# Mixture-of-experts encoder: the last expert's last 512 columns brought to their tokens by products with a matrix of ones

## The chip, the cores and the metric

One core of one Trainium2 chip. The metric is device microseconds (us) for one execution of the whole program. TensorE is called PE here (PEld is its weight load), VectorE DVE, ScalarE ACT, GpSimd POOL, and SyncE SP; SPq and POOLq are the queues in which SP and POOL issue transfers.

## The reference, cut to what matters

A two-layer encoder on 512 tokens of width 1024. Attention and the dense feed-forward of layer 0 are the same in both kernels. What the change touches is the end of layer 1: a mixture of 8 experts, of which each token takes 2.

```python
def _moe(h, router_w, router_b, w1, w3, w2):
    logits = (hf @ router_w) + router_b
    top_logits, top_idx = lax.top_k(logits, 2)
    gates = softmax(top_logits)
    # each expert e on the rows x of its tokens:
    y = (silu(x @ w1[e]) * (x @ w3[e])) @ w2[e]      # 1024 -> 2816 -> 1024
    out[token] += gate * y                           # two experts per token
...
x = layernorm(ALPHA * x + g2 * moe(h), ln2_g, ln2_b)  # the output, 512 x 1024
```

## The kernel before

**Places.** The router ranks the experts by how many tokens they have and gives each a *place* with a fixed number of rows, `SLOT = [336, 320, 128, 128, 64, 64, 64, 64]`; what doesn't fit goes to 7 spare blocks of 128 rows, computed at the very end under a condition (`tc.If(n_ovv > 0)`). Each of the 4 blocks of 128 tokens has, for its 2 experts, a row number in `dst` (as float in `dstf`) and a gate in `gw`.

**Two lanes.** `lane_big` computes places 0 and 1, `lane_small` the other six; their steps are interleaved by hand by shares of work. Every float32 product is made of three (`mm3`) or two products of parts, high (`wh`) and low (`wl`); ACT makes the high part of each weight tile (L111) and DVE the low (L113). Place 1 (320 rows, blocks of 128, 128 and 64) is the last work of the program. Its last product, with the second half of the inner dimension, is cut by columns into `PIECES = [(0, 512), (512, 256), (768, 256)]`. `out_turned` (L1504) computes a piece with columns on the partitions and adds it into `part` on DVE (L1525, scaled by `g2col`). `turn_back` (L1529) transposes it on PE (L1533), copies it from the PSUM bank on ACT (L1535) and stores it in DRAM (L1542), in `ybuf`, which is three tensors, one for each piece.

**Combine.** When a piece's rows are stored, `Final.combine(i)` (L1665) fetches, for each of 4 blocks of tokens and each of the 2 experts, 128 rows of that piece by an indirect transfer from POOL (L1679); DVE multiplies by the gate and adds to the residual `us` (L1681) and takes statistics (L1684). That is 8 gathers for a piece, 24 in all. For the last piece the normalisation follows, block by block: mean and variance (L310), the root on ACT (L312, L313) and DVE (L314 to L317), one pass over 128x1024 on DVE (L1687), and a second one: for two of the blocks on ACT (L1689) and POOL (L1690), for the other two on DVE (L1692). Then the block is stored (L1693).

**Order.** At build time a planner writes one list of instructions for each engine, with costs of its own; a line of the source that is ready in its plan can move ahead of earlier ones, unless `order(after, before)` forbids it. On the chip each engine runs its list in that order. In `combine` the adds are ordered behind the last write of `part` (`order(j, first)`, `first = last_out[0]`). Tiles with one `tag` share `bufs` buffers: `ye` and `hs` have 3 each, the PSUM tag `pt` has 2 and `ps` 6.

Of the kernel before, what the change touches and what calls it, by code (L numbers as in the profile page):

```python
# [18 lines left out]
D = 1024  # L19
# [37 lines left out]
def build(tc, I, out, dbg=None, upto=99):  # L57
# [1008 lines left out]
    G.memset(zero, 0.0)  # L1066
    zeros = [(y, SLOT_ROWS + i * P) for i in range(N_OVER) for y in ybuf]
    js = ExitStack()
    jobs = mod_steps(js.enter_context(tc.tile_pool(name="jp", bufs=1, side="right")), [(0, 5, None), (1, 1, 1.0), (1, 0, 0.0), (1, 2, None), (1, 4, 1.0), (1, 3, 0.0), (1, 5, None)])
    for f in range(FT):  # L1070
        pp_ = []
        for _ in range(4):
            next(jobs, None)
        for y, r in zeros[f:f + 1]:
            SP.dma_start(y[r:r + P, :], zero[:, :y.shape[1]])
        for w in ("ffn_w1", "ffn_w3"):
# [398 lines left out]

    last_out = [None]
    g2col = modcol[1, 5]

    def out_part(ew2, lhs, c0, nc_, store, late=None):
# [19 lines left out]
        z = pz if gl is not None else halves(pz, nc_)  # L1499
        last_out[0] = V.tensor_tensor(y[:m, :nc_], z[:m, :nc_], g2row[:m, c0:c0 + nc_], op=OP.mult)  # L1500
        store(0, c0, nc_, y[:m, :nc_])
        yield 1

    def out_turned(ew2, lhs, part, c0, nc_, fs, first):  # L1504
# [3 lines left out]
        for c in range(c0, c0 + nc_, 256):  # L1508
# [11 lines left out]
            for i in range(2):  # L1520
                m = c // P + i
                if first:
                    A.activation(part[:, m, :], pz[i][:, :n], AF.Copy, scale=g2col[:, m:m + 1])
                else:
                    last_out[0] = V.scalar_tensor_tensor(part[:, m, :], pz[i][:, :n], g2col[:, m:m + 1],  # L1525
                                                         part[:, m, :], op0=OP.mult, op1=OP.add)
# [11 lines left out]
    def stores(row):  # L1538
        def f(i, c0, nc_, y):
            for (b0, bn), buf in zip(PIECES, ybuf):  # L1540
                if c0 <= b0 < c0 + nc_:
                    SP.dma_start(buf[row(i, y.shape[0]), :], y[:, b0 - c0:b0 - c0 + bn])  # L1542
        return f
# [75 lines left out]
    def lane_big():  # L1619
        for s, nxt in zip(lanes[0], lanes[0][1:] + (None,)):  # L1620
# [29 lines left out]

    class Final:

        def prepare(self):
# [10 lines left out]

        def combine(self, i):  # L1665
            c0, n = PIECES[i]
            last = i == len(PIECES) - 1
            table = exp_table() if last else None
            ys = []
            for tag, k in ((("geh", 5), ("gel", 3)), (("xeh", 4), ("xel", 4)), (("xg", 4), ("xg", 4)))[i]:  # L1670
                y = xp.tile([P, k, n], F32, name=nm("yg"), tag=tag, bufs=XG if tag == "xg" else 1)
                ys += [y[:, j, :] for j in range(k)]
            first = last_out[0]
            for t in range(NT):
                u = self.us[t]
                uc = u[:, c0:c0 + n]
                for k in range(2):
                    y = ys[2 * t + k]
                    G.indirect_dma_start(out=y, out_offset=None, in_=ybuf[i],  # L1679
                                         in_offset=bass.IndirectOffsetOnAxis(ap=dst[:, t, k:k + 1], axis=0))  # L1680
                    j = V.scalar_tensor_tensor(uc, y, gw[:, k, t:t + 1], uc, op0=OP.mult, op1=OP.add)  # L1681
                    if first is not None:
                        order(j, first)
                V.bn_stats(self.sts[t][:, i, :], uc)  # L1684
                if last:
                    mean, r = ln_stat(xp, self.sts[t], table)
                    V.scalar_tensor_tensor(u, u, mean, self.lg, op0=OP.subtract, op1=OP.mult)  # L1687
                    if t < 2:
                        A.activation(u, u, AF.Copy, scale=r)  # L1689
                        G.tensor_tensor(u, u, self.lb, op=OP.add)  # L1690
                    else:
                        V.scalar_tensor_tensor(u, u, r, self.lb, op0=OP.mult, op1=OP.add)  # L1692
                    SP.dma_start(out[0, t * P:(t + 1) * P, :], u)  # L1693

# [20 lines left out]
    fin.combine(len(PIECES) - 1)  # L1715

# [3 lines left out]
    with tc.If(n_ovv > 0):  # L1720
        with tc.For_i(0, n_ovv, 1) as i:
# [14 lines left out]
        last_out[0] = None  # L1736
        again = Final()
        again.prepare()
        for i in range(len(PIECES)):
            again.combine(i)  # L1740
    ms.close()
# [25 lines left out]
```

## Time and profile before

| | |
|---|---|
| time before, median of 3 runs | 2538.1 us (2535.07 to 2540.49) |
| the profiled execution: its own time | 2537.35 us |
| its span, first to last instruction | 2535.5 us |
| outside the span | 1.85 us |
| busy: PE / DVE / ACT / POOL | 96% / 70% / 56% / 17% |
| mean granted clock of PE | 0.986 of full speed |

The span counts from the first instruction of the profiled execution; what lies around it, 1.85 us, is the difference to that execution's own time. Times in the rows below are us from the span's start. PE is busy nearly always, but a share over the whole span says nothing of the end, where PE has no work left.

### The profile page before, as it was taken

What the parts mean: (1) busy time and instruction counts of PE and PEld (TensorE: products, weight loads), DVE (VectorE), ACT (ScalarE), POOL (GpSimd) and SP (SyncE); (2) the same over time, 40 slices, a digit from 0 to 9 for tenths busy, and PEclk for the clock granted to TensorE, in tenths of its full rate; (3) what the DMA queues carried; (4) which work ended last, traced back from release to release, by engine and by line L of the source; (5) the groups of instructions that cost most, each with busy time, mean ns of one, the idle gap of its engine ahead of it and who ended that gap; (6) DMA issues with size and microseconds to landing.
All of it is one profiled execution on the core that took longest, in us unless ns stands there. A gap on an engine that the chain in (4) does not pass through costs nothing.

```text
span 2535.5 us, 37048 instructions
## 1 busy us (share of the span) xinstructions
PE 2436.4 (96%) x13124; PEld 2081.7 (82%) x13124; DVE 1779.1 (70%) x2788; ACT 1432.5 (56%) x2320; POOL 430.0 (17%) x393
## 2 busy tenths in 40 slices
PE   8999999998999999999999997999999999999994
PEld 6878877787788888878877876888899999999994
DVE  3688776647665335687775366977788888888875
ACT  3577774223222224677764225666677777777761
POOL 1423330001000502323326004400000000000004
PEclk9999999999999999999999998999999999999997
DMA  8322225746866433222226329998999999999993
GB/s 228 92 59 71 73 74 191 229 137 213 281 217 194 150 100 111 75 67 72 79 67 196 96 75 276 313 338 275 315 318 297 323 286 319 333 303 331 291 337 122
DMA packets 453210, 502.20 MB, mean 198 GB/s; under 512 B 19314, under 2 KB 322920, under 8 KB 453016
## 3 DMA queue, kind: packets, MB, share of 16 engines
q1 hardware_dynamic: 437616, 453.64, 57.1%
q0 software_dynamic: 13888, 45.30, 5.1%
q8 instruction: 105, 1.72, 0.3%
q10 hardware_dynamic: 1512, 0.81, 0.1%
q14 instruction: 89, 0.73, 0.1%
HBM read 474.95 MB, written 24.74 MB: 197 GB/s over the span
## 4 chain that ended last, share of the span: by engine, by line
PE 79%; DVE 7%; DMA 6%; ACT 5%; issue 2%; POOL 1%; SPq 0%; ACTq 0%; DVEq 0%; POOLq 0%
PE ps L127 21%; PE ps L128 20%; PE ps L129 20%; PE ps L1371 5%; PE ps L1372 5%; PE pt L444 2%; DMA ws<-in_moe_w 2%; DMA mst<-in_w_ada 1%; DVE wl L113 1%; ACT wh L111 1%; PE ps L732 1%; PE ps L733 1%; DMA ol<-o_dram 1%; DVE ps L745 1%; DMA ws<-in_w_in 1%
## 5 line engine op out<-in xcount | busy, mean ns | idle before, releaser
L111 ACT ACTIVATE wh<-ws 128x1024 fp32r<-128x1024 f32 (+3 forms) x786 | 779.0, 1011 | 688.5 <-PE ps L128 342.9
L113 DVE TENSOR_TENSOR wl<-ws,wh 128x1024 fp32r<-128x1024 f32 (+3 forms) x712 | 836.2, 1193 | 356.4 <-ACT wh L111 348.5
L129 PE MATMUL ps<-hTh,wl 128*128 128x512 f32 (+1 forms) x904 | 347.5, 385 | 4.4 <-DVE wl L113 4.4
L128 PE MATMUL ps<-hTl,wh 128*128 128x512 f32 (+1 forms) x904 | 349.3, 387 | 0.8 <-POOL hTl L282 0.8
L127 PE MATMUL ps<-hTh,wh 128*128 128x512 f32 (+1 forms) x904 | 349.7, 387 | 0.1
L127 PE MATMUL ps<-x3h,wh 128*128 128x336 f32 (+1 forms) x704 | 221.2, 314 | 0.0
L129 PE MATMUL ps<-x3h,wl 128*128 128x336 f32 (+1 forms) x704 | 220.3, 313 | 0.0
L128 PE MATMUL ps<-x3l,wh 128*128 128x336 f32 (+1 forms) x704 | 219.9, 312 | 0.0
L113 POOL TENSOR_TENSOR wl<-ws,wh 128x1024 fp32r<-128x1024 f32 (+1 forms) x74 | 179.3, 2430 | 216.0 <-ACT wh L111 148.0
L129 PEld LDWEIGHTS ps<-hTh,wl 128*128 128x128 f32 x904 | 171.6, 190 | 37.9 <-DVE wl L113 5.3
L127 PEld LDWEIGHTS ps<-hTh,wh 128*128 128x128 f32 x904 | 171.6, 190 | 35.4 <-issue 2.9
L128 PEld LDWEIGHTS ps<-hTl,wh 128*128 128x128 f32 x904 | 171.5, 190 | 32.9 <-POOL hTl L282 2.0
L1371 PE MATMUL ps<-wh,xes 128*128 128x512 f32 (+1 forms) x384 | 143.3, 378 | 0.0
L1372 PE MATMUL ps<-wl,xes 128*128 128x512 f32 (+1 forms) x384 | 141.4, 374 | 0.0
L127 PEld LDWEIGHTS ps<-x3h,wh 128*128 128x128 f32 x704 | 132.3, 188 | 3.4
L128 PEld LDWEIGHTS ps<-x3l,wh 128*128 128x128 f32 x704 | 132.4, 188 | 3.0
L129 PEld LDWEIGHTS ps<-x3h,wl 128*128 128x128 f32 x704 | 132.1, 188 | 0.2
L127 PE MATMUL ps<-wh,hTh 128*128 128x256 f32 (+1 forms) x384 | 116.5, 305 | 1.8 <-DVE dq L519 1.1
L214 DVE SCALAR_TENSOR_TENSOR macc<-mst,condrep,macc 128x1024 f32<-128x1024 f32 x70 | 89.8, 1282 | 35.7 <-DMA mst<-in_w_ada 35.0
L128 PE MATMUL ps<-wl,hTh 128*128 128x256 f32 (+1 forms) x384 | 114.0, 298 | 0.8 <-DVE wl L113 0.8
L129 PE MATMUL ps<-wh,hTl 128*128 128x256 f32 (+1 forms) x384 | 113.4, 297 | 0.0
L124 DVE TENSOR_TENSOR pTl<-pt,pTh 128x512 fp32r<-128x512 f32 x128 | 86.5, 685 | 36.1 <-ACT pTh L123 35.5
(428 smaller groups left out, 5371.2 us busy)
## 6 DMA issues: line engine op xcount, KB each, us to landing
ws<-in_moe_w SPq DMA_DIRECT2D x492, 512.0 KB, 5.8
ws<-in_w_in SPq DMA_DIRECT2D x94, 512.0 KB, 3.9
mst<-in_w_ada SPq DMA_DIRECT2D x80, 512.0 KB, 4.8
ws<-in_ffn_w SPq DMA_DIRECT2D x66, 512.0 KB, 4.0
ws<-in_moe_w SPq DMA_DIRECT2D x48, 256.0 KB, 3.8
wa<-in_w_ada SPq DMA_DIRECT2D x16, 512.0 KB, 6.4
ws<-in_w_br_diff SPq DMA_DIRECT2D x16, 512.0 KB, 3.7
ws<-in_w_out SPq DMA_DIRECT2D x16, 512.0 KB, 3.8
```

Source lines behind the costliest of these rows:

```text
L111: A.activation(h, st, AF.Copy)
L113: i = eng.tensor_tensor(l, st, h, op=OP.subtract)
L124: V.tensor_tensor(l, src, h, op=OP.subtract)
L127: T.matmul(o, ah, bh, start=start, stop=False)
L128: T.matmul(o, ah, bl, start=False, stop=False)
L129: last_mm[0] = T.matmul(o, al, bh, start=False, stop=stop)
L214: i = V.scalar_tensor_tensor(acc, st, condrep[:, k, 0:1], acc, op0=OP.mult, op1=OP.add)
L444: T.transpose(pt[:, t * P:(t + 1) * P], tiles[t][:, k * P:(k + 1) * P], ident)
L732: T.matmul(scs[m], q[:, m, tt], k[:, m], start=True, stop=False)
L733: last_mm[0] = T.matmul(scs[m], q[:, m, tt], kl[:, m], start=False, stop=True)
L1371: T.matmul(o, xs, wh, start=start, stop=False)
L1372: T.matmul(o, xs, wl, start=False, stop=stop)
```

## The change

`ybuf` becomes two tensors of 512 columns (`BUFS`). The rows of place 1 in the second one are filled with zeros early (during the dense feed-forward of layer 0), so that a gather from it brings the other experts' part alone and need not wait for place 1. `others` issues 16 gathers of 512 columns, the second half's first; it also builds `ones`, three tiles of 128 x 512 with a one where a row of place 1 belongs to a token (compare on DVE, transpose on PE, copy on ACT), and `gate`, the gate of that token for place 1. `adds` does the adds of one half, interleaved with the steps of `out_turned` for the second and the third piece. `scatter` replaces `turn_back` and `combine` for these two pieces: it transposes the piece back, splits it into high and low, multiplies both with `ones` into PSUM (24 products of 256 columns a piece) and adds the sum times `gate` to `us`. The normalisation is done for two blocks at a time (`norm`), its last block stored in two halves. The rows of place 1 are still stored, behind that, for the conditional part, which repeats the combine with 16 gathers.

```diff
+BUFS = [(0, 512), (512, 512)]
-    ybuf = [dram.tile([N_ROWS, n], F32, name=f"ybuf{i}") for i, (_, n) in enumerate(PIECES)]
+    ybuf = [dram.tile([N_ROWS, n], F32, name=f"ybuf{i}") for i, (_, n) in enumerate(BUFS)]
...
-    zeros = [(y, SLOT_ROWS + i * P) for i in range(N_OVER) for y in ybuf]
+    zeros = [(y, SLOT_ROWS + i * P, P) for i in range(N_OVER) for y in ybuf]
+    zeros += [(ybuf[1], SLOT[0] + i, min(P, SLOT[1] - i)) for i in range(0, SLOT[1], P)]
...
-                    yield from out_turned(ew[2], g[1], part, c0, nc_, (FH, FT), False)
-                    turn_back(part, SLOT[s], c0, nc_, row_stores(s))
-                    if nxt is None and i > 0:
-                        fin.combine(i - 1)
+                        fin.others(s)
+                    work = out_turned(ew[2], g[1], part, c0, nc_, (FH, FT), False)
+                    if nxt is not None or i == 0:
+                        yield from work
+                        turn_back(part, SLOT[s], c0, nc_, row_stores(s))
+                    else:
+                        adds = fin.adds(2 - i, fin.ys[2 - i])
+                        for n in work:
+                            yield n
+                            next(adds, None)
+                        for _ in adds:
+                            pass
+                        fin.scatter(s, i, c0, part)
...
+        def gathers(self, i, idx, tags):
...
+            for t in range(NT):
+                for k in range(2):
+                    G.indirect_dma_start(out=ys[2 * t + k], out_offset=None, in_=ybuf[i],
+                                         in_offset=bass.IndirectOffsetOnAxis(ap=idx[:, t, k:k + 1], axis=0))
+            return ys
+
+        def others(self, s):
...
+            late = self.gathers(1, dst, (("geh", 5), ("gel", 3)))
+            self.ys = [self.gathers(0, dst, (("xeh", 2), ("xel", 2), ("xg", 2), ("xg", 2))), late]
...
+            for t in range(NT):
+                p1 = xp.tile([P, 512], F32, name=nm("ye"), tag="ye", bufs=YE)
+                V.tensor_scalar(p1[:, :n], rows[:, :n], dstf[:, t, 0:1], None, op0=OP.is_equal)
+                V.scalar_tensor_tensor(p1[:, :n], rows[:, :n], dstf[:, t, 1:2], p1[:, :n], op0=OP.is_equal, op1=OP.add)
+                pt = psum_t()
+                for b, m in enumerate(blocks(n)):
+                    T.transpose(pt[:m, b * P:(b + 1) * P], p1[:, b * P:b * P + m], ident)
+                for b, m in enumerate(blocks(n)):
+                    A.activation(self.ones[b][:m, t * P:(t + 1) * P], pt[:m, b * P:(b + 1) * P], AF.Copy)
+
+        def adds(self, i, ys):
+            c0, n = BUFS[i]
+            for t in range(NT):
+                first = last_split[0]
+                uc = self.us[t][:, c0:c0 + n]
+                for k in range(2):
+                    j = V.scalar_tensor_tensor(uc, ys[2 * t + k], gw[:, k, t:t + 1], uc, op0=OP.mult, op1=OP.add)
+                    if first is not None:
+                        order(j, first)
+                if i == 0:
+                    V.bn_stats(self.sts[t][:, 0, :], uc)
+                yield
+
+        def scatter(self, s, i, c0, part):
...
+                        T.transpose(pt[:m, (b - b0) * 256 + j * P:(b - b0) * 256 + (j + 1) * P],
+                                    part[:, c0 // P + j, b * P:b * P + m], ident)
+                split(h[:m, w], l[:m, w], pt[:m, w])
...
+            for t0 in range(0, NT, 2):
+                pz = psum()
+                for t in (t0, t0 + 1):
+                    o = pz[:, (t - t0) * 256:(t - t0 + 1) * 256]
+                    for b, (m, h, l) in enumerate(hl):
+                        one = self.ones[b][:m, t * P:(t + 1) * P]
+                        T.matmul(o, one, h, start=(b == 0), stop=False)
+                        T.matmul(o, one, l, start=False, stop=(b == len(hl) - 1))
+                    uc = self.us[t][:, c0:c0 + 256]
+                    V.scalar_tensor_tensor(uc, o, self.gate[:, t:t + 1], uc, op0=OP.mult, op1=OP.add)
+                    V.bn_stats(self.sts[t][:, i, :], uc)
+                if last:
+                    self.norm((t0, t0 + 1), 3, table)
...
+        def norm(self, ts, n, table):
...
+            for j, t in enumerate(ts):
+                u = self.us[t]
+                V.scalar_tensor_tensor(u, u, mv[:, j, 0:1], self.lg, op0=OP.subtract, op1=OP.mult)
+                if t < 2:
+                    A.activation(u, u, AF.Copy, scale=r[:, j:j + 1])
+                    G.tensor_tensor(u, u, self.lb, op=OP.add)
+                    SP.dma_start(out[0, t * P:(t + 1) * P, :], u)
+                else:
+                    for c in HALVES if t == NT - 1 else [(0, D)]:
+                        c = slice(c[0], c[0] + c[1])
+                        V.scalar_tensor_tensor(u[:, c], u[:, c], r[:, j:j + 1], self.lb[:, c], op0=OP.mult, op1=OP.add)
+                        SP.dma_start(out[0, t * P:(t + 1) * P, c], u[:, c])
```

## Rows read from the trace of the kernel before

**Rows 1.** Windows: length, busy us (instructions) of each engine, PE clock, DMA.

```profile
2476.60:2498.95 22.35, 22.35 (x153) 21.39 (x151) 12.07 (x18) 4.62 (x8) 10.88 (x11) 1.00 0.49 148
2498.95:2535.50 36.55, 1.37 (x8) 0.54 (x6) 23.09 (x53) 5.11 (x13) 19.03 (x16) 0.57 0.36 121
```

**Rows 2.** The chain that ended last, its end: start, us, what.

```profile
2492.63 3.75 DMA yg<-ybuf,r
...
2501.74 4.56 DMA ybuf<-ye
2507.09 1.19 POOL yg L1679
```

**Rows 3.** Timeline of PE: start, us (pipelined, so starts give the pace).

```profile
1284.05 0.28 PE L127 MATMUL ps<-wh,hTh 128*128 128x256 f32 x1
1284.17 0.28 PE L128 MATMUL ps<-wl,hTh 128*128 128x256 f32 x1
...
2476.85 0.91 PE L1533 MATMUL pt<-ident,part 128*128 128x128 f32 x6
```

**Rows 4.** Timeline of DVE, the last pieces and the tail.

```profile
2488.02 1.01 DVE L1525 SCALAR_TENSOR_TENSOR part<-ps,mcol,part 128x320 f32<-128x320 f32 x2 [4.12 <-PE ps L129]
...
2490.03 2.14 DVE L1681 SCALAR_TENSOR_TENSOR fu<-yg,r,fu 128x512 f32<-128x512 f32 x3 [0.35 <-DMA yg<-ybuf,r]
2492.09 1.27 DVE L1684 BATCH_NORM_STATS2 fst<-fu 128x6 f32<-128x512 f32 x2
...
2498.95 0.98 DVE L1525 SCALAR_TENSOR_TENSOR part<-ps,mcol,part 128x320 f32<-128x320 f32 x2
...
2507.78 0.48 DVE L1681 SCALAR_TENSOR_TENSOR frows<-yg,r,frows 128x256 f32<-128x256 f32 x1
2508.18 0.42 DVE L1684 BATCH_NORM_STATS2 fst<-fu 128x6 f32<-128x256 f32 x1
...
2518.88 1.99 DVE L1681 SCALAR_TENSOR_TENSOR frows<-yg,r,frows 128x256 f32<-128x256 f32 x1
...
2523.38 1.51 DVE L317 TENSOR_TENSOR bmv<-bmv 128x1 f32<-128x1 f32 x1
...
2527.94 1.28 DVE L1692 SCALAR_TENSOR_TENSOR frows<-frows,bmv 128x1024 f32<-128x1024 f32 x1
```

**Rows 5.** Timeline of POOL, its gathers and its two passes of the normalisation.

```profile
2483.12 1.65 POOL L1679 DMA_INDIRECT yg<-ybuf,r  x1 [22.99 <-DMA ybuf<-ye]
...
2517.97 2.61 POOL L1690 TENSOR_TENSOR fu<-fu,frows 128x1024 f32<-128x1024 f32 x1
2522.20 2.67 POOL L1690 TENSOR_TENSOR fu<-fu,frows 128x1024 f32<-128x1024 f32 x1 [1.61 <-ACT fu L1689]
```

**Rows 6.** Timeline of ACT, the tail.

```profile
2500.40 0.66 ACT L1535 ACTIVATE ye<-pt 128x256 f32<-128x256 f32 x2 [9.48 <-PE pt L1533]
...
2516.69 1.15 ACT L1689 ACTIVATE fu<-fu,bmv 128x1024 f32<-128x1024 f32 x1 [2.97 <-DVE bmv L317]
2517.75 0.28 ACT L312 ACTIVATE bmv<-bmv,eps_ln 128x1 f32<-128x1 f32 x1
```

**Rows 7.** Groups by line and form: a split out of PSUM, whole run.

```profile
L124 DVE TENSOR_TENSOR pTl<-pt,pTh 128x512 fp32r<-128x512 f32 x128 | 86.5, 685 | 36.1 <-ACT pTh L123 35.5
...
L123 ACT ACTIVATE pTh<-pt 128x512 fp32r<-128x512 f32 x128 | 74.2, 591 | 51.5 <-PE pt L444 51.2
```

**Rows 8.** DMA issues from 2455 on: count, KB each, median us to landing.

```profile
ybuf<-ye SPq DMA_DIRECT2D x2, 256.0 KB, 2.2
out<-frows SPq DMA_DIRECT2D x1, 512.0 KB, 3.8
```

**Rows 9.** Windows behind PE's last transposes, columns as in rows 1.

```profile
2501.50:2503.00 1.50, 0.00 (x0) 0.00 (x0) 1.11 (x4) 0.21 (x1) 1.19 (x2) 1.00 0.91 277
2503.00:2505.00 2.00, 0.00 (x0) 0.00 (x0) 0.50 (x2) 0.00 (x0) 1.39 (x2) 0.82 0.42 128
2505.00:2508.00 3.00, 0.00 (x0) 0.00 (x0) 1.50 (x4) 0.00 (x0) 1.41 (x2) 0.50 0.32 92
```

More of the change, by code (lines that the diff above doesn't have):

```diff
@@ L1073, in build @@
             next(jobs, None)
-        for y, r in zeros[f:f + 1]:
-            SP.dma_start(y[r:r + P, :], zero[:, :y.shape[1]])
+        for y, r, m in zeros[f:f + 1]:
+            SP.dma_start(y[r:r + m, :], zero[:m, :y.shape[1]])
         for w in ("ffn_w1", "ffn_w3"):
@@ L1539, in f @@
         def f(i, c0, nc_, y):
[L1540 to L1542 removed]
+            for (b0, bn), buf in zip(BUFS, ybuf):
+                if b0 <= c0 < b0 + bn:
+                    SP.dma_start(buf[row(i, y.shape[0]), c0 - b0:c0 - b0 + nc_], y)
         return f
@@ new lines, in others @@
+        def others(self, s):
+            r, n = starts[s], SLOT[s]
+            here, lt = et([P, NT, 2]), et([P, NT, 2])
+            V.tensor_scalar(here, dstf, r - 0.5, None, op0=OP.is_gt)
+            V.tensor_scalar(lt, dstf, r + n - 0.5, None, op0=OP.is_lt)
+            V.tensor_tensor(here, here, lt, op=OP.mult)
+            late = self.gathers(1, dst, (("geh", 5), ("gel", 3)))
+            self.ys = [self.gathers(0, dst, (("xeh", 2), ("xel", 2), ("xg", 2), ("xg", 2))), late]
+            gs = et([P, NT, 2])
+            V.tensor_tensor(gs, here, gw.rearrange("p k t -> p t k"), op=OP.mult)
+            self.gate = et([P, NT])
+            V.tensor_reduce(self.gate, gs, axis=AX.X, op=OP.add)
+            rows = xp.tile([P, 512], F32, name=nm("rows"), tag="hs", bufs=3)
+            G.iota(rows[:, :n], pattern=[[1, n]], base=r, channel_multiplier=0, allow_small_or_imprecise_dtypes=True)
+            self.ones = [xp.tile([P, S], F32R, name=nm("one"), tag=tag, bufs=b) for tag, b in (("eg", 2), ("eg", 2), ("xm", 1))]
+            for t in range(NT):
[7 more added lines that the diff above has]
+                    A.activation(self.ones[b][:m, t * P:(t + 1) * P], pt[:m, b * P:(b + 1) * P], AF.Copy)
@@ L1667, in combine @@
+        def scatter(self, s, i, c0, part):
+            n = SLOT[s]
+            bl = blocks(n)
             last = i == len(PIECES) - 1
             table = exp_table() if last else None
[L1669 to L1673, printed above, removed]
@@ L1674, in combine @@
-            for t in range(NT):
[L1675 to L1693, printed above, removed]
+            pts, hl = [], []
@@ new lines, in scatter @@
+            for b0 in range(0, len(bl), 2):
+                pt = psum_t()
+                h, l = (xp.tile([P, 512], F32R, name=nm("hs"), tag=tag, bufs=3) for tag in ("hs", "ye"))
+                bs = list(enumerate(bl))[b0:b0 + 2]
+                m = bs[0][1]
+                for b, mb in bs:
+                    assert mb == m
+                    for j in range(2):
+                        T.transpose(pt[:m, (b - b0) * 256 + j * P:(b - b0) * 256 + (j + 1) * P],
+                                    part[:, c0 // P + j, b * P:b * P + m], ident)
+                w = slice(0, 256 * len(bs))
+                split(h[:m, w], l[:m, w], pt[:m, w])
+                pts.append((bs, pt))
+                for b, mb in bs:
+                    hl.append((m, h[:m, (b - b0) * 256:(b - b0 + 1) * 256], l[:m, (b - b0) * 256:(b - b0 + 1) * 256]))
@@ new lines, in scatter @@
+            for bs, pt in pts:
+                m = bs[0][1]
+                y = xp.tile([P, 512], F32, name=nm("ye"), tag="ye", bufs=YE)
+                A.activation(y[:m, :256 * len(bs)], pt[:m, :256 * len(bs)], AF.Copy)
+                for b, mb in bs:
+                    row_stores(s)(b, c0, 256, y[:m, (b - bs[0][0]) * 256:(b - bs[0][0] + 1) * 256])
+        def norm(self, ts, n, table):
+            k = len(ts)
+            mv = xp.tile([P, k, 2], F32, name=nm("fmv"), tag="fmv", bufs=2)
+            for j, t in enumerate(ts):
+                V.bn_aggr(mv[:, j, :], self.sts[t][:, :n, :].rearrange("p a b -> p (a b)"))
+            w = xp.tile([P, 4, k], F32, name=nm("fw"), tag="fw", bufs=2)
+            v, r0, q, r = (w[:, j, :] for j in range(4))
+            V.tensor_scalar(v, mv[:, :, 1], LN_EPS, None, op0=OP.add)
+            order(A.activation(r0, v, AF.Ln), table)
+            A.activation(r0, r0, AF.Exp, scale=-0.5)
+            V.scalar_tensor_tensor(q, r0, -0.5, r0, op0=OP.mult, op1=OP.mult)
+            V.tensor_tensor(q, q, v, op=OP.mult)
+            V.scalar_tensor_tensor(r, q, 1.5, r0, op0=OP.add, op1=OP.mult)
+            for j, t in enumerate(ts):
+                u = self.us[t]
[9 more added lines that the diff above has]
+                        SP.dma_start(out[0, t * P:(t + 1) * P, c], u[:, c])
@@ L1695, in build, with anew @@
+        def anew(self):
+            table = exp_table()
+            last_split[0] = None
+            tags = (("geh", 5), ("gel", 3)), (("xeh", 2), ("xel", 2), ("xg", 2), ("xg", 2))
+            for i in range(len(BUFS)):
+                for _ in self.adds(i, self.gathers(i, dst, tags[i])):
+                    pass
+            for t in range(NT):
+                V.bn_stats(self.sts[t][:, 1, :], self.us[t][:, 512:])
+                self.norm((t,), 2, table)
     fin = Final()
@@ L1735, in build @@
                     pass
-        last_out[0] = None
         again = Final()
         again.prepare()
-        for i in range(len(PIECES)):
-            again.combine(i)
+        again.anew()
     ms.close()
```

12 lines of the change are left out of this document (6 added, 6 removed).

## Prediction, made before the changed kernel ran

> **What bounds the kernel now.** I read the windows first, for the last two stretches. In the 22.35 us before 2498.95 PE is busy for all 22.35, at full clock; in the 36.55 us from there to the end it is busy for 1.37 [rows 1]. So PE bounds up to 2498.95, and whatever is added to PE before that moves the end by its own length; behind it lies a tail in which PE has nothing to do. I call 2498.95 T0: there DVE begins to scale the last piece, straight behind the last product [rows 4].
>
> The chain of waits says what sets the tail: the store of the last piece takes 4.56 us to land, POOL starts the first gather at 2507.09 and then issues eight, and DVE takes them one by one [rows 2]. The timeline of DVE ends it: its last pass starts at 2527.94 and lasts 1.28, to 2529.22 [rows 4]; the store of 512 KB lands 3.8 later [rows 8], at 2533.0, and 2.5 us follow to the end of the span, 2535.5. The tail is 30.3 us to DVE's end and 6.3 behind it.
>
> **What goes.** Store, gathers and their landing are no longer between the last product and the normalisation. I don't subtract them; I build the new tail from T0 on, since DVE's own work then comes to the front.
>
> **What PE gets before the last product.** 12 transposes for the ones, at 0.91 us for six [rows 3]: 1.8. The second piece's 24 products of 256 columns, at 0.12 a start [rows 3]: 2.9. Its six transposes stood there before. PE has no idle time to hide them [rows 1], so both count: 4.7, and T0' is 2503.65. Below: 4.3, were the transposes 0.12 each. Above: what PE waits for in that place (rivals).
>
> What covers the rest up to T0': the 16 gathers. Each takes POOL about 1.2 us, 20 us in all; those of the second half need only the small lane's stores, those of the first the first piece's, as now (2483.12 [rows 5]). Today the last of eight lands at 2492.63 + 3.75 = 2496.4 [rows 2], 7 us ahead of T0'. DVE's added work is the second half's eight adds (0.71 each [rows 4]: 5.7), eight compares of 320 columns (an add of 256 takes 0.48 [rows 4], so about 0.6 each: 4.8), and the second piece's split and sums. DVE was busy 12.07 of 22.35 us [rows 1], so it has room, but most of the second half of that room is wanted (rivals). The 12 copies on ACT, 4.62 busy there [rows 1], cost nothing. The zero stores (17, not 21) and nine row stores fewer are far from the end, where no wait of rows 2 lies: nothing.
>
> **The tail, from T0'.** (1) DVE's scaling and the transposes: ACT starts on the transposed piece 1.45 after T0 today (2500.40 [rows 6]), and the same now. High part of 512 columns 0.59, low part 0.69 [rows 7], the last block's low part of 256 columns about half, 0.35; the product that follows, 0.28 [rows 3]; with hops 3.6 for the first block of tokens. Four blocks on DVE at 0.40 (start to start) plus 0.42 [rows 4], 0.8 each: 6.8; the aggregates of the first pair fit between, 0.4: 7.2. PE is done with all 24 products (0.72 a block) before that, at 5.8.
> (2) Root and its DVE steps of the first pair, 0.4; first pass of its two blocks, 1.3 each (1.28 [rows 4]): 10.2.
> (3) ACT then scales those blocks, 1.15 each, and takes the second pair's root, 0.28 a step [rows 6]. ACT works its list in order; if the root stands behind both scalings, it ends at 10.2 + 1.15 + 0.5 = 11.85, and DVE waits 1.65. I keep the wait, since the source has that order; ahead of them it is 0.
> (4) Second pair: steps 0.4, two first passes 2.6, one second pass 1.3, the last block in halves 0.7 each: 17.55.
> (5) The passes on POOL. Today a DVE add that starts at 2518.88 takes 1.99 instead of about 0.48, and ends at 2520.87, just behind POOL's pass (2517.97 + 2.61 = 2520.58); a step of one column takes 1.51 and ends at 2524.89, with POOL's second (2524.87) [rows 4, 5]. Two such stalls cost 1.5 + 1.4 = 2.9, and DVE has two-input work beside both passes again: 20.45. Without overlap 0.
> (6) Behind DVE's end: the last store is 256 KB instead of 512. Stores of 256 KB landed in 2.2, the one of 512 in 3.8 [rows 8]; I take 2.9, and 2.5 as now: 5.4 (4.7 to 6.3).
> DVE's end is T0' + 20.45, 2524.1, the span's end 2529.5, 6.0 us earlier than now. The profiled execution took 2537.35, 1.85 more than its span, so 2531.3. The median of the runs shown is 0.75 above it: 2532.0. Own range: (3) at 0 and half of (5) give 2528.9, a PE or DVE slip of 2 to 3 us gives 2535: 2529 to 2535.
>
> To the stalls of (5) the Trainium skill has a rule ("SBUF — State Buffer", section "SBUF: two separate sides"): VectorE and GpSimd share a port pair that is an exclusive lock, and a VectorE instruction with two SBUF inputs blocks wholly while a GpSimd one that reads SBUF holds it. The two rows above agree, 0.29 and 0.02 us apart from the end of POOL's pass. By it the sum would hold up to both passes in full, which is the third rival below, in place of the stalls measured.
>
> **The rivals.**
> *A shorter tail.* The planner puts the second pair's root ahead of the scalings and POOL's passes fall beside DVE's one-input work: minus 1.65 and minus 2.9, 2527.5. For it: DVE takes the blocks' work in another order than the source's (two statistics together behind three adds [rows 4]). Against: POOL's second pass waits for ACT today [rows 5], so both come as late as the scalings do.
> *PE waits in the last piece.* Between the second piece's scaling (2488.02 [rows 4]) and T0' DVE has 1.0 of scaling, 5.7 of adds, 2.5 of statistics (1.27 a pair [rows 4]), 1.1 of splitting and 3.2 of sums, 13.5 of 15.6 us, while the gathers come in until 2496.4. Waiting for them in list order, it slips; PE, which works in order too, waits for the split and T0' moves. From a slip of 2.1 it eats the gain; 3 to 6 give 2535 to 2538, no change.
> *POOL holds DVE for both passes whole.* Issued one behind the other they block DVE 2.6 + 2.7 [rows 5] instead of 2.9: 2534.4. Against: a pass of the two begins while a DVE pass runs and does not stop it.
> *Slower: adds planned ahead of the piece's scaling.* The adds were held behind the last write of `part`; now only behind a weight split. If all the first half's stand before the second piece's scaling in DVE's list, that waits until 2496.4 + 0.7 = 2497.1 instead of 2488.02 to 2489, and PE behind it, 8.1 us: 2540.1. Today PE does nothing from 2501.5 on; the granted clock was 1.00 until 2503, 0.82 up to 2505 and 0.50 behind [rows 9], half of full, 1.2 of 2.4 GHz. If it fell so here, the last piece (2488.02 to 2498.95, 10.9 [rows 4]) would take as long again: up to 2551. It decides if the clock falls in that wait. Against: the first gather is issued at 2483.12 [rows 5] and the adds of eight are not ready at once.
>
> **How the numbers follow.** What a measurement of this kernel can tell from no change is 0.2%, 5.1 us: faster ends at 2533.0, slower begins at 2543.2. The forecast 0.45 (0.35 of it below 2533.0), shorter tail 0.18 (all faster), PE waits 0.18 (no change), POOL whole 0.10 (0.03 faster), slower one 0.09 (0.07 beyond 2543.2, 0.02 below). Faster 0.35 + 0.18 + 0.03 = 0.56; same 0.10 + 0.18 + 0.07 + 0.02 = 0.37; slower 0.07. The range reaches from the shorter tail with transposes at 0.12 each and the store at its lower bound, 2526.5, to the upper end of PE's waits with a store at its upper bound, 2539; what is left out is the slower rival and the ends of the others.
>
> **What would show it.** Right: all 16 gathers issued before the last product; PE busy without a gap up to about 2503.6; ACT's split 1.45 behind that, DVE's first sum out of PSUM at 3.6, its last pass ending about 20 us behind T0', PE's 24 products there at the full clock. Each step wrong: gaps in PE between the second piece's transposes and its products (a slip, or in the worst case the clock at half in the last piece); a wait of DVE on ACT's root other than 1.65; DVE's steps of 1.5 us and more beside POOL's passes, more or fewer than two. The prediction falls if T0' moves by over 7 us, or if the tail to DVE's end is under 16 or over 23 us.

## The result, and the profile after

| | before | after |
|---|---|---|
| time, median (lowest to highest) | 2536.59 us (2534.53 to 2540.49), 4 runs | 2556.91 us (2556.69 to 2556.97), 4 runs |
| ratio after / before, 95% interval | | 1.0079 [1.0066, 1.0091] |
| the profiled execution: its own time / its span | 2537.35 / 2535.5 us | 2556.96 / 2555.2 us |
| mean granted clock of PE | 0.986 | 0.982 |

Slower by 0.8%, 20 us, where 2532.0 us (2526.5 to 2539.0) and "faster" were forecast. The median lies 18 us above the upper end of the range.

First the two stretches of [rows 1], cut at the same places of the program: from the first piece's second scaling (where it would have begun, see below) to the last piece's scaling, T0', and from there to the end. The columns are those of rows 1.

```profile
2475.10:2526.24 51.14, 35.82 (x188) 32.20 (x187) 27.59 (x47) 7.69 (x21) 15.32 (x15) 0.73 0.34 97
2526.24:2555.20 28.96, 8.60 (x33) 5.89 (x31) 17.97 (x31) 4.73 (x10) 5.70 (x2) 0.56 0.23 87
```

The stretch before T0' took 22.35 us with PE busy all the time [rows 1]; now it takes 51.14, PE is busy for 35.82 of them, and the mean granted clock is 0.73. The tail is shorter, 28.96 instead of 36.55. So the tail did give something, 7.6 us, and the stretch ahead of it lost 28.8. (The two differences make 21.2; the execution reached this place 1.5 us earlier.) PE is no longer what bounds the stretch before T0', which was the first sentence of the prediction's reading. The waits from 2460 on name what does, with total us, times, longest:

```profile
POOL yg L1684 <- DMA ybuf<-ye: 25.7, 2, 13.8
PEld pt L1535 <- DVE part L1527: 12.1, 1, 12.1
DVE fu L1722 <- DMA yg<-ybuf,r: 11.3, 7, 7.6
DVE frows L1722 <- DMA yg<-ybuf,r: 4.1, 2, 2.1
```

PE waits once, 12.1 us, for a piece's scaling on DVE; DVE waits nine times for gathers, 15.4 us in all; POOL waits for stores before it can gather. The same place on DVE's timeline, with the scalings (L1527) between the adds (L1722):

```profile
2465.42 1.01 DVE L1527 SCALAR_TENSOR_TENSOR part<-ps,mcol,part 128x320 f32<-128x320 f32 x2
...
2475.66 0.75 DVE L1722 SCALAR_TENSOR_TENSOR fu<-yg,r,fu 128x512 f32<-128x512 f32 x1 [7.59 <-DMA yg<-ybuf,r]
...
2484.17 0.75 DVE L1722 SCALAR_TENSOR_TENSOR frows<-yg,r,frows 128x512 f32<-128x512 f32 x1 [2.15 <-DMA yg<-ybuf,r]
...
2486.24 1.22 DVE L114 TENSOR_TENSOR wl<-ws,wh 128x1024 fp32r<-128x1024 f32 x1
2487.38 1.00 DVE L1527 SCALAR_TENSOR_TENSOR part<-ps,mcol,part 128x320 f32<-128x320 f32 x2
...
2503.49 1.00 DVE L1527 SCALAR_TENSOR_TENSOR part<-ps,mcol,part 128x320 f32<-128x320 f32 x2
...
2507.07 0.75 DVE L1722 SCALAR_TENSOR_TENSOR frows<-yg,r,frows 128x512 f32<-128x512 f32 x1 [1.92 <-DMA yg<-ybuf,r]
2507.74 1.01 DVE L125 TENSOR_TENSOR hs<-pt,hs 128x512 fp32r<-128x512 f32 x2
...
2526.24 1.01 DVE L1527 SCALAR_TENSOR_TENSOR part<-ps,mcol,part 128x320 f32<-128x320 f32 x2 [6.61 <-PE ps L130]
```

The first piece has 512 columns, scaled in two halves. Before, the second half's scaling came 9.68 us behind the first's (at 2476.61); here it would have come at 2465.42 + 9.68 = 2475.10, and came at 2487.38. In between stand the eight adds of the second half of the columns, one by one, five of them with a wait for their gather: DVE stood idle for 7.6 us before the first and 2.15 before the sixth. They need nothing of place 1, and stand in DVE's list ahead of a scaling whose operands had long been there. A smaller copy of it comes later: the second piece's split (L125) at 2507.74 stands behind an add that waited 1.92.

What PE made of it, on its timeline and in windows (columns as in rows 1):

```profile
2475.69 0.39 PE L128 MATMUL ps<-g3h,wh 128*128 128x320 f32 x1
2487.98 0.69 PE L1535 MATMUL pt<-ident,part 128*128 128x128 f32 x2 [11.90 <-DVE part L1527]
...
2504.18 1.02 PE L1744 MATMUL pt<-ident,part 128*128 128x128 f32 x6 [2.05 <-DVE fu L1722]
```

```profile
2470.00:2475.00 5.00, 5.00 (x36) 5.00 (x35) 0.00 (x0) 1.14 (x2) 2.01 (x3) 1.00 0.23 67
...
2480.00:2485.00 5.00, 0.00 (x0) 0.00 (x0) 2.37 (x5) 0.00 (x0) 2.68 (x4) 0.50 0.67 197
2485.00:2490.00 5.00, 2.02 (x9) 1.98 (x10) 4.51 (x6) 0.55 (x2) 0.00 (x0) 0.50 0.00 0
...
2495.00:2500.00 5.00, 5.00 (x38) 4.79 (x37) 3.38 (x6) 2.50 (x13) 3.90 (x4) 1.00 0.44 118
...
2510.00:2515.00 5.00, 5.00 (x17) 3.96 (x17) 2.38 (x5) 0.00 (x0) 0.00 (x0) 0.50 0.15 49
```

PE's list has the transposes of the first piece there, so PE stood for 11.90 us with the second piece's products behind them. The granted clock went from 1.00 to 0.50 in that gap, 2.4 to 1.2 GHz, and stayed there for some microseconds of work behind it. After the wait of 2.05 at 2504.18 it fell again: the second piece's 24 products ran at half clock, with 17 matmuls in 5 us at 2510 where 38 ran at 2495. A busy share of 5.00 of 5.00 doesn't show that; the column of the clock does.

Why the gathers came so late stands in the chain of waits:

```profile
2460.18 11.39 DMA ybuf<-ye
...
2472.38 1.00 POOL yg L1684
```

The small lane's last rows were given to SP's queue at 2460.18, straight behind weight tiles, and took 11.39 us to land; only then could POOL issue its first gather. The queue's own timeline has the weight tiles just ahead of it:

```profile
2457.45 2.50 SPq L102 DMA_DIRECT2D ws<-in_moe_w  x2
```

In the kernel before, stores of that tensor took 2.2 [rows 8].

The tail, from T0' = 2526.24, on DVE and POOL:

```profile
2530.63 0.48 DVE L1760 SCALAR_TENSOR_TENSOR fu<-ps,r,fu 128x256 f32<-128x256 f32 x1 [1.04 <-PE ps L1758]
...
2541.55 2.10 DVE L1783 SCALAR_TENSOR_TENSOR fw<-fw 128x2 f32<-128x2 f32 x1
2543.68 2.27 DVE L1784 TENSOR_TENSOR fw<-fw 128x2 f32<-128x2 f32 x1
...
2547.38 1.41 DVE L1796 SCALAR_TENSOR_TENSOR frows<-frows,fw 128x512 f32<-128x512 f32 x2
```

```profile
2540.23 5.70 POOL L1791 TENSOR_TENSOR fu<-fu,frows 128x1024 f32<-128x1024 f32 x2 [34.25 <-DVE fu L1788]
```

First sum 4.39 behind T0' (3.6 in the prediction), end of DVE 2548.79, 22.55 behind T0' (20.45), span's end 6.4 behind that (5.4). Two steps on two columns each, which take 0.15 where nothing holds them, take 2.10 and 2.27 and end inside and at the end of POOL's two passes.

### The profile page after: what moved, and what is told of

Same layout as the page of the kernel before. It is cut to its first block, busy times and chain, and to the rows that moved or that the text cites. A ratio compares the mean times of both kernels' runs of the same rounds, so it can differ in the third digit from the quotient of the medians.

```text
span 2555.2 us, 37171 instructions
## 1 busy us (share of the span) xinstructions
PE 2454.2 (96%) x13184; PEld 2093.9 (82%) x13184; DVE 1787.6 (70%) x2798; ACT 1434.1 (56%) x2330; POOL 421.9 (17%) x386
## 4 chain that ended last, share of the span: by engine, by line
PE 79%; DVE 8%; DMA 5%; ACT 4%; issue 2%; POOL 1%; SPq 0%; ACTq 0%; DVEq 0%; POOLq 0%
PE ps L128 20%; PE ps L129 20%; PE ps L130 20%; PE ps L1374 5%; PE ps L1375 5%; PE pt L445 2%; DVE wl L114 1%; DMA mst<-in_w_ada 1%; PE ps L733 1%; PE ps L734 1%; ACT wh L112 1%; DMA ol<-o_dram 1%; DVE ps L746 1%; DMA ybuf<-ye 1%; ACT ps L742 1%
## 5 line engine op out<-in xcount | busy, mean ns | idle before, releaser
L129 PE MATMUL ps<-g3l,wh 128*128 128x336 f32 (+1 forms) x352 | 112.4, 319 | 0.0
L128 PE MATMUL ps<-g3h,wh 128*128 128x336 f32 (+1 forms) x352 | 112.2, 319 | 0.0
```

The lines of the kernel that those rows point to most:

```text
L128: T.matmul(o, ah, bh, start=start, stop=False)
L129: T.matmul(o, ah, bl, start=False, stop=False)
```

## The experiments

Two theories stood at the start, and the expectations name them so. **W**: the order of DVE's list is the cause; the adds of the second half and, for a smaller part, those of the first wait for gathers and stand ahead of a piece's scaling or split. **L**: DVE and PE simply have too much added work there, and the order is not the cause. A third explanation is not named there, and numbers 4 and 6 bear on it: **S**, the late store, and with it the late gathers, is the cause by itself, in whatever order. Where two runs are compared below, the ratios to before are, since each group of runs has its own runs of before.

**1. The second half's adds behind the first piece's scaling.**

```diff
+    last_out = [None]
...
-                    V.scalar_tensor_tensor(part[:, m, :], pz[i][:, :n], g2col[:, m:m + 1],
+                    last_out[0] = V.scalar_tensor_tensor(part[:, m, :], pz[i][:, :n], g2col[:, m:m + 1],
...
+            behind_ = (last_out[0] if i == 1 else None) if last_split[0] is not None else None
...
-                    if first is not None:
-                        order(j, first)
+                    for o in (first, behind_):
+                        if o is not None:
+                            order(j, o)
```

> The eight adds of the second half are held, in DVE's list, behind the scaling of the first piece; nothing else changes by hand. Theory W (DVE stands at adds whose gathers have not landed, and the first piece's scaling, and PE with it, stand behind them): the gap of PE from 2475.9 to 2488.0 goes, and with it the stretch at half clock behind it, 12 + 3 us; the first half's adds still stand ahead of the second piece's scaling and cost a few us there: 2540 to 2546 us. Rival L (DVE and PE simply have too much added work there, and the order is not the cause): the gap is filled with the same work elsewhere, 2553 to 2558 us.

Measured: 2543.78 us (2539.21 to 2549.48, 8 runs), ratio 1.0031 [1.0020, 1.0042]. One ordering rule takes back 0.5 of the 0.8%, as W expected, with DVE's and PE's work unchanged; L's 2553 us is not reached. DVE's scaling stands at its place, 9.67 behind the first half's, though the first gather is hardly earlier (2470.77, 6.45 behind the first scaling; 6.96 in the changed kernel):

```profile
2473.99 1.01 DVE L1528 SCALAR_TENSOR_TENSOR part<-ps,mcol,part 128x320 f32<-128x320 f32 x2
...
2510.70 1.01 DVE L1528 SCALAR_TENSOR_TENSOR part<-ps,mcol,part 128x320 f32<-128x320 f32 x2 [3.80 <-PE ps L130]
```

W holds for the greater part: with the gathers as late as that, the gap of 11.9 us is gone. A new gap of 5.1 stands further on; PE's timeline shows where:

```profile
2485.97 0.87 PE L1712 MATMUL pt<-ident,ye 128*128 128x128 f32 x3 [5.13 <-DVE ye L1709]
```

The transposes of the ones wait for DVE's compares, and these stand behind the waiting adds. It is the same fault one step later.

**2. The first half's adds behind the second piece's sums, the second half's as they were.**

```diff
+            behind_ = (self.summed if i == 0 else None) if last_split[0] is not None else None
...
-                    V.bn_stats(self.sts[t][:, i, :], uc)
+                    self.summed = V.bn_stats(self.sts[t][:, i, :], uc)
```

> The eight adds of the first half are held behind the second piece's sums out of PSUM; the second half's adds stay where they were. Theory W: the first gap of PE stays, the second one (from 2502.1 on) and the waits in the second piece's products shrink: 5 to 9 us less, 2548 to 2552 us. Rival L: no change, 2555 to 2558 us, since the adds take the same time later.

Measured: 2552.46 us (2550.78 to 2554.14, 2 runs), ratio 1.0065 [1.0045, 1.0085], 0.5 above W's range. PE's first gap is as it was, 11.6 us; the second piece's split no longer stands behind an add. So the first half's adds are the smaller part, about 0.14% (3.6 us) by the ratios, though the intervals overlap.

**3. Both.**

```diff
+            behind_ = (last_out[0] if i == 1 else self.summed) if last_split[0] is not None else None
```

> Both of the above. Theory W: no gap of over 1 us is left in PE before the last product, which ends at about 2502 to 2505 as predicted; the tail stays as it is in the changed kernel, 22.6 to DVE's end and 6.4 behind: span about 2532, 2531 to 2537 us. Rival L: 2550 us or more.

Measured: 2543.46 us (2541.28 to 2549.94, 7 runs), ratio 1.0032 [1.0016, 1.0048], no better than number 1; 2531 to 2537 was expected, and missed by over 6. What had not been counted is the gap at the ones' transposes (`5.14` at 2486.49, as in number 1) and the half clock behind it (0.50 from 2486 to 2490). From the first piece's second scaling to T0' number 3's profile takes 35.91 us and number 1's 36.71. With the first half's adds behind the sums, DVE comes to T0' straight from an add's statistics, with no wait for PE ahead of it:

```profile
2509.79 0.68 DVE L1729 BATCH_NORM_STATS2 fst<-frows 128x6 f32<-128x512 f32 x1
2510.41 1.01 DVE L1528 SCALAR_TENSOR_TENSOR part<-ps,mcol,part 128x320 f32<-128x320 f32 x2
```

So DVE has no slack left there, but it isn't late: PE's last product starts 0.09 behind the scaling, as in number 1, where DVE had waited 3.80 for PE. PE's timeline of number 3, then of number 1:

```profile
2510.50 0.31 PE L130 MATMUL ps<-g3h,wl 128*128 128x320 f32 x1
```

```profile
2510.79 0.31 PE L130 MATMUL ps<-g3h,wl 128*128 128x320 f32 x1
```

**4. The small lane's last store on ACT's queue, all else as changed.** DVE's, PE's and POOL's lists stay in their order.

```diff
-                    SP.dma_start(buf[row(i, y.shape[0]), c0 - b0:c0 - b0 + nc_], y)
+                    (q or SP).dma_start(buf[row(i, y.shape[0]), c0 - b0:c0 - b0 + nc_], y)
...
-        return stores(lambda i, n: slice(starts[s] + i * P, starts[s] + i * P + n))
+        return stores(lambda i, n: slice(starts[s] + i * P, starts[s] + i * P + n), A if s == lanes[1][-1] else None)
```

> The order on DVE, PE and POOL stays that of the changed kernel; only the two stores of the small lane's last place go out from ACT's queue instead of SP's, where they stood behind weight loads and took 11.4 us to land. Theory W: POOL's first gather starts as the store lands, some 4 us after its issue (2465 to 2467 instead of 2472.4), so DVE's first add starts 5 to 8 us earlier and PE's first gap shrinks by as much, less half clock behind it: 2546 to 2551 us. Rival L: the gathers come earlier and the time stays, 2554 to 2558 us. If the store lands no earlier from that queue, both give no change and the run tells nothing.

Measured: 2551.11 us (2550.35 to 2551.87, 2 runs), ratio 1.0060 [1.0040, 1.0080], at the upper end of W's range. The store went out at 2458.79; its landing isn't in that trace. The first gather came 6.9 us behind it, where the changed kernel took 12.2:

```profile
2465.68 1.88 POOL L1684 DMA_INDIRECT yg<-ybuf,r  x1 [8.46 <-DVE part L1527]
```

That is 1.65 behind the first scaling instead of 6.96, and the second scaling came at 2481.57, 7.9 late instead of 12.3. S is right that the store is late and that it costs: 0.19% by the ratios (4.8 us), whose intervals overlap, with no time of either kernel within the other's range. But with the gathers 5.3 us earlier the adds still hold the scaling for 7.9: the lateness feeds the fault, the order makes it.

What the store itself takes is seen in later runs, with the time to landing in the last place: number 5 (SP's queue), then number 6 (ACT's).

```profile
ybuf<-ye SPq DMA_DIRECT2D x1, 128.0 KB, 11.4
```

```profile
ybuf<-ye ACTq DMA_DIRECT2D x1, 128.0 KB, 6.3
```

Numbers 7 and 9, from ACT's queue too, have 5.7 and 6.4. In these four runs and in the changed kernel the first gather starts 0.81 behind the landing; an estimate from that for number 4 is 6.1. The Trainium skill ("DMA: Bandwidth & Descriptors", section "Queues, rings and completion order") says that SP and ACT each own a row of rings on the same 16 DMA engines, which consume each ring's descriptors in order and take turns between rows. The landing times agree with that: behind weight tiles in SP's row 11.39 in the changed kernel, in ACT's own row 6.3 in number 6, though the DMA engines were no less busy there: their share was 0.89 over the 11.39 us, and 1.02 over the 6.28 us (number 6, columns as in rows 1):

```profile
2461.26:2467.54 6.28, 6.28 (x45) 6.28 (x44) 3.21 (x5) 2.03 (x3) 0.00 (x0) 1.00 1.02 392
```

**5. Number 3, with the ones built ahead of the gathers, their compares in buffers of their own.**

```diff
-            late = self.gathers(1, dst, (("geh", 5), ("gel", 3)))
-            self.ys = [self.gathers(0, dst, (("xeh", 2), ("xel", 2), ("xg", 2), ("xg", 2))), late]
...
-                p1 = xp.tile([P, 512], F32, name=nm("ye"), tag="ye", bufs=YE)
+                if t % 2 == 0:
+                    p2 = xp.tile([P, 2, 512], F32, name=nm("cmp"), tag=("xeh", "xel")[t // 2], bufs=1)
+                p1 = p2[:, t % 2, :]
...
+            late = self.gathers(1, dst, (("geh", 5), ("gel", 3)))
+            self.ys = [self.gathers(0, dst, (("xeh", 2), ("xel", 2), ("xg", 2), ("xg", 2))), late]
```

> The order of the run with both halves held behind, and the matrix of ones is built first: compares, transposes and copies stand ahead of the gathers in the source, the compares in four buffers of their own instead of three that the row stores hold. Theory W (what is left is again PE standing at work whose DVE part is queued behind adds that wait for gathers: 5.1 us at the transposes of the ones): that gap goes, the last product ends at 2504 to 2506, 4 to 7 us less than the run with both held: 2535 to 2539 us. Rival D (DVE as a whole is full there, so that the adds of the first half end no earlier and the last scaling waits for them): under 2 us less, 2540 to 2543 us.

Measured: 2537.86 us (2532.18 to 2544.79, 10 runs), ratio 1.0002 [0.9990, 1.0013]: as before the change. The gap at the ones is gone. With three edits of order and none of work, 0.77 of the 0.79% are back.

**6. Number 5 with number 4's store.**

> As the run with the ones early, and the last small place's two stores go out from ACT's queue. Theory W: the gathers of the second half start 5 to 6 us earlier and DVE waits less for them, but PE had no gap left that came of it: within 1.5 us of the run with the ones early. Rival D (DVE is the limit up to the last scaling): 2 to 4 us less, since DVE's waits for these gathers become time for the rest.

Measured: 2536.24 us (2533.68 to 2539.79, 10 runs), ratio 0.9994 [0.9984, 1.0003], within the intervals the same as number 5. So in the right order the late store costs nothing that stands clear of the noise, and S falls as a cause by itself. It isn't without effect: in number 5's profile, the slowest of its ten, PE waits 1.16 us for the second piece's scaling, in number 6's 0.29. W expected 1.5 us at most between the two and rival D 2 to 4; the medians give 1.6, the ratios 2.0, so this run doesn't settle that.

This kernel is also the cleanest test of the prediction's sum. From the first piece's second scaling to T0' it takes 29.16 us (2476.17 to 2505.33), 22.34 before, 27.05 predicted: 2.1 more than the sum. PE's timeline has them:

```profile
2489.79 1.02 PE L1748 MATMUL pt<-ident,part 128*128 128x128 f32 x6 [0.29 <-DVE part L1528]
2491.40 0.51 PE L1761 MATMUL ps<-hs,one 128*128 128x256 f32 x2 [0.58 <-ACT hs L124]
...
2494.43 0.28 PE L1761 MATMUL ps<-hs,one 128*128 128x256 f32 x1
2494.55 0.28 PE L1762 MATMUL ps<-hs,one 128*128 128x256 f32 x1
...
2494.99 0.38 PE L1761 MATMUL ps<-hs,one 64*128 64x256 f32 x1
2495.21 0.28 PE L1762 MATMUL ps<-hs,one 64*128 64x256 f32 x1
2495.42 0.41 PE L130 MATMUL ps<-g3h,wl 128*128 128x320 f32 x1
...
2505.43 0.31 PE L130 MATMUL ps<-g3h,wl 128*128 128x320 f32 x1
```

PE waits twice, 0.9 in all. The second piece's 24 products take 4.2 from start to start, not 2.9: those of the last block of place 1, of 64 rows, start 0.21 to 0.22 apart, where the sum had 0.12 for all. The 12 transposes for the ones take 1.2, not 1.8. That makes 1.6; the other 0.5 is not traced. The last product starts 0.10 behind T0', as in numbers 1 and 3, so DVE isn't late here either. The tail is as in the changed kernel, 22.6 to DVE's end.

**7. Number 6 with all second passes of the normalisation on DVE.**

```diff
-                if t < 2:
-                    A.activation(u, u, AF.Copy, scale=r[:, j:j + 1])
-                    G.tensor_tensor(u, u, self.lb, op=OP.add)
-                    SP.dma_start(out[0, t * P:(t + 1) * P, :], u)
-                else:
+                if True:
```

> As the run before it (ones early, store from ACT's queue), and all four blocks take their second pass of the normalisation on DVE; ACT's scaling and POOL's passes of two blocks go. Theory P (DVE's steps of 2.10 and 2.27 us stand still while POOL's two passes run): 4.1 us of standing go, two passes of 1.2 come, and the stores are nearer together: 1 to 3 us less than the run before it. Rival: those steps are slow for another reason, and 2.4 us are added.

Measured: 2532.57 us (2529.75 to 2538.87, 10 runs), ratio 0.9988 [0.9978, 0.9998], 3.7 us under number 6 by the medians, 1.5 by the ratios, whose intervals overlap. The two profiled executions took the same time (2536.40 and 2536.12 us), since this one came to T0' 3.8 later, so only their tails are compared. On DVE's timeline, number 6 and then this one:

```profile
2520.72 2.10 DVE L1787 SCALAR_TENSOR_TENSOR fw<-fw 128x2 f32<-128x2 f32 x1
2522.85 2.27 DVE L1788 TENSOR_TENSOR fw<-fw 128x2 f32<-128x2 f32 x1
```

```profile
2521.32 2.47 DVE L1796 SCALAR_TENSOR_TENSOR fu<-fu,fw,frows 128x1024 f32<-128x1024 f32 x2
...
2524.98 0.15 DVE L1787 SCALAR_TENSOR_TENSOR fw<-fw 128x2 f32<-128x2 f32 x1
2525.16 0.16 DVE L1788 TENSOR_TENSOR fw<-fw 128x2 f32<-128x2 f32 x1
```

Two small steps that took 4.37 take 0.31; the two passes that DVE gets cost 2.47. That is 1.6 of the tail's gain of 3.6 in these two profiles (22.6 to 19.0). Some 1.8 more lie ahead of the passes, at the products, which ran at the full clock here and at half in number 6 from 2510 on. The full clock doesn't need this edit: the tails of numbers 1 and 5, with POOL's passes, had it too, and there DVE ends 20.9 behind T0', 1.9 above number 7.

**8. Number 7 with a PSUM bank for each block's sum**, not one for two blocks.

```diff
-                pz = psum()
...
-                    o = pz[:, (t - t0) * 256:(t - t0 + 1) * 256]
+                    o = psum()[:, :256]
```

> As the run before it, and each block of tokens has a PSUM bank of its own for its sum, where two blocks shared one. Theory B (the products of the second block of a pair wait until DVE has read the first): DVE's waits of 0.7, 1.25 us and more between the four sums shrink to what six products take, 0.5 to 2 us less. Rival: PE's products at half clock set the pace alone: no change beyond 0.5 us.

Measured: 2532.61 us (2530.27 to 2536.48, 10 runs), ratio 0.9985 [0.9975, 0.9994]. The same as number 7; the shared bank costs nothing that can be measured.

**9. Number 7 with six products of 512 columns ahead of each piece's sums, into a bank that nobody reads**, to keep PE at work while the split goes on.

```diff
+            pd = psum()
+            for _ in range(6):
+                T.matmul(pd, self.ones[0][:, :P], self.ones[0], start=True, stop=True)
             for t0 in range(0, NT, 2):
```

> The run with the normalisation on DVE (shared banks, store from ACT's queue, ones early), and six more products of 512 columns with the ones, whose result nobody reads, ahead of each piece's products, where PE waits for DVE and ACT. Theory C (PE's short idle stretches around the two scatters let the granted clock fall to half in some executions, so that the 24 products and what stands behind them take twice as long): the clock stays at full up to the last product, and the time lies 0 to 2 us below the run without them, with less spread. Rival: the six products stand in the way of the transposes and cost 0.5 to 1.5 us, and the clock falls as before.

Measured: 2533.29 us (2529.75 to 2537.82, 12 runs), ratio 0.9983 [0.9974, 0.9992]. No gain over number 7, and by the ratios the rival's cost of 0.5 to 1.5 us doesn't show either. The windows of its tail, from T0' = 2509.62 on:

```profile
2510.00:2515.00 5.00, 4.37 (x25) 3.15 (x23) 2.32 (x6) 1.46 (x3) 0.00 (x0) 1.00 0.07 24
2515.00:2520.00 5.00, 3.73 (x14) 2.63 (x13) 3.97 (x11) 0.57 (x2) 0.00 (x0) 0.55 0.16 47
```

In this execution the clock fell all the same, with PE busy for 3.73 of the 5 us.

**10. The kernel before, with all second passes on DVE**, and nothing of the change.

```diff
-                    if t < 2:
-                        A.activation(u, u, AF.Copy, scale=r)
-                        G.tensor_tensor(u, u, self.lb, op=OP.add)
-                    else:
-                        V.scalar_tensor_tensor(u, u, r, self.lb, op0=OP.mult, op1=OP.add)
+                    V.scalar_tensor_tensor(u, u, r, self.lb, op0=OP.mult, op1=OP.add)
```

> The kernel before, with the second pass of all four blocks on DVE as in the run with the normalisation on DVE; nothing of the change. It tells how much of that run's advantage is this edit alone. If POOL's passes cost the kernel before the two stalls of 2.9 us that its rows show, less the two passes of 1.2 that come: 0.5 us less up to 1 us more, 2535 to 2537 us. If it gains 3 us as in the changed kernel, nothing of the advantage is left to the change.

Measured: 2538.49 us (2532.84 to 2544.72, 12 runs), ratio 1.0008 [0.9998, 1.0018]; 2535 to 2537 was expected. The edit of number 7 gains nothing without the change. So the 0.12 to 0.17% of numbers 7 to 9, whose intervals all end below 1, come from the change in the right order together with that edit. These three are the versions that beat both kernels; the gain is below the 0.2% that the prediction set as its bound.

## Why the prediction was wrong

**The step that failed** is the paragraph "What covers the rest up to T0'". It costed 16 gathers, 16 adds and their statistics, and eight compares at nothing, since POOL has the time, the second half's gathers "need only the small lane's stores", and DVE "has room". The busy share was right and was no answer: DVE took the scaling at 2487.38, behind eight adds that waited for gathers, though its operands were there 12.3 us earlier: what waits in its list holds what stands behind. T0' came at 2526.24 instead of 2503.65, 22.6 of the 25.7 us by which the span missed its forecast of 2529.5. They split at the first piece's second scaling: this came at 2487.38, 12.3 later than it could, less the 1.5 that the execution was ahead (10.8); from it to T0' it took 38.9 instead of 27.05 (11.8). Of those 11.8, 4.3 us of work at half clock from 2488 to 2492 cost about half their length, the wait at 2504.18 cost 2.05, and the rest is mostly the half clock from 2506 to 2519.6. Shown by runs are the order of the adds (1), of the compares (1, 3 and 5) and the store (4); this last split is read from one profile.

**The slower rival** named the mechanism, "adds planned ahead of the piece's scaling", and the clock behind it, and had 0.09. It looked for it at the smaller of the two places, the first half's adds and the second piece's scaling (PE's wait of 2.05 at 2504.18), with the argument that eight adds are not ready at once. The second half's adds are what the change set free: in the planner's list they are ready early, and on the chip they were not. With up to 2551 even that rival was too low, since it counted one piece's wait and the change has two places for it. The remark "now only behind a weight split" had the fact on which all turned; the diff shows it, and the price of it wanted more than a chance in ten.

**PE's added work** was put at 4.7, and number 6, with the order mended, has 6.8 more than before on that way: the products were priced 1.3 too low, the ones' transposes 0.6 too high, and 0.9 are waits. Those waits are all that came of the rival *PE waits in the last piece*; number 6 measured no change (0.9994), as that rival forecast, but only in part by its mechanism. Its span, 2534.3, is 4.8 above the forecast of 2529.5: 1.7 lie up to T0', 2.2 in the tail, 0.9 behind DVE's end.

**The tail.** It took 22.55 for 20.45 to DVE's end, and most of the excess is the clock, which the prediction expected full. It fell to half at 2530; in numbers 1 and 5, where it stayed at 1.00 over these products, DVE ends 20.9 behind T0':

```profile
2510.70:2518.00 7.30, 6.14 (x33) 4.13 (x31) 4.61 (x10) 1.83 (x4) 0.00 (x0) 1.00 0.11 36
```

```profile
2526.24:2536.96 10.72, 8.60 (x33) 5.89 (x31) 6.36 (x16) 1.83 (x4) 0.00 (x0) 0.67 0.09 29
```

These are PE's last 33 matmuls, from T0' on, in number 1 and then in the changed kernel. (1) and (2): 12.0 to the end of the first pair's first passes, 10.3 in number 1, 10.2 in the sum; the first sum came at 4.39, at 4.17 in number 1, not 3.6. (3): the wait for the second pair's root is 0.1, not 1.65, though ACT did take the root behind both scalings (at 2541.09); DVE did the second pair's first passes meanwhile. (5): the stalls are 4.1, not 2.9, two steps of 0.15 that lasted 2.10 and 2.27: POOL's passes came one behind the other, as in the rival *POOL holds DVE for both passes whole*, which had 5.3. That (3) and (5) miss in opposite directions, by 1.5 and 1.2, is luck. The rule cited in the prediction ("SBUF — State Buffer", section "SBUF: two separate sides", of the Trainium skill) agrees: the second step ends at 2545.95, 0.02 behind POOL's 2545.93, and where POOL has no pass (number 7) the two take 0.15 and 0.16. (6): 6.4, not 5.4, just above the upper bound; the smaller last store brought nothing (6.3 before, 6.3 in number 7).

**Right** were T0' as the time from which the tail is counted, the 16 gathers issued before the last product (the last at 2504.70), ACT's split 1.7 behind T0' (1.45), and that the tail gets shorter, though from 36.55 to 28.96 and not to the sum's 25.85.

## What to carry to other kernels

When a dependence is removed, look at what else it did: here the old rule that held the adds behind the last write of a piece also kept them out of the way of that piece's scaling. In an engine's list, every instruction that waits for a transfer is costed by what stands behind it and by which engine waits for that, not by the engine's busy share; place it behind all that TensorE needs, even where a plan says that its data are there earlier. A small store whose landing starts a chain is better not queued behind weight tiles: here that cost 0.19% in the wrong order, and nothing clear of the noise in the right one.

## What the hardware did unexpectedly

- A store on SP's queue behind weight tiles landed in 11.39 us, a store of the same rows on ACT's queue in 6.3 (number 6), with the DMA engines busy in both cases (share 0.89 over the 11.39 us, 1.02 over the 6.28).
- The granted clock of PE fell to 0.50 behind short waits with work on both sides. In the changed kernel it was 0.50 for 13.6 us from 2506 on, in which PE was busy for 12.81. The products of the tail ran at 1.00 throughout in the profiles of numbers 1, 5, 7 and 8, and fell to 0.50 on the way in the changed kernel and in numbers 2, 3, 4, 6 and 9; nothing in the rows tells why. Numbers 6 and 7 have the same list of products. So have numbers 5 and 6, and the second piece's products ran at 0.50 in number 5 (2500 to 2505) and at 1.00 in number 6 (2490 to 2498); there PE had waited 1.16 us for the piece's scaling in number 5 and 0.29 in number 6. Whether that wait is the reason no run shows.
- Products of 256 columns over 64 rows started 0.21 to 0.22 us apart at the full clock, those over 128 rows 0.12 (number 6).
- A step of two columns on DVE took 2.27 us beside a POOL pass over other data, and 0.16 without one (number 7).
